# Six gate blocks of each layer computed with the first six mixer units instead of in the merge

## The chip, the cores and the metric

The kernel runs on one core of a Trainium2 chip. The metric is device time in microseconds for one execution of the whole program, the median of three runs. TensorE (PE) multiplies, VectorE (DVE), ScalarE (ACT) and GpSimd (POOL) do the element-wise work, and SyncE (SP) issues every DMA.

## The reference, cut to what matters

Two layers of a hybrid backbone over 640 tokens (512 latent, 128 prompt) of width 1024. In each layer the normed input h is projected once; the columns feed three token mixers (A, B, C) and 24 gate blocks of 128 channels (8 for each branch).

```
z = h @ w_in_l
gates = sigmoid(g + b_gate_l)                       # 3 branches x 1024 channels
y = gates[:, :, 0] * (oa @ w_ba) + gates[:, :, 1] * (ob @ w_bb) + gates[:, :, 2] * (oc @ w_bc)
x = x + mp[2] * (y @ w_o)                           # then an MLP of the squared ReLU
```

A gate block depends on h alone. It is needed only where the branch product of the same 128 channels is multiplied by it.

## The kernel before, in words

Every product is computed to nearly float32: both operands are split into a high and a low float32r part, and three matmuls (high x high, high x low, low x high) make one. A block of 128 output channels over 640 tokens with 8 input blocks is therefore 8 x 3 x 2 = 48 matmuls, one of 256 and one of 384 columns in each pair (`HALVES`, `product`, lines 34 and 818).

**Weights** come in one stream in the order of use (`Stream`, line 535): `_program` gives its order, `load` fetches a piece of up to 768 columns, `make` splits pieces of 384 columns into high (ACT, `act`) and low. In the mixers the low part is made by POOL (`ws.lo = "POOL"`, lines 1290 and 1311), in the merge and the MLP by DVE (line 1341). The split pieces live in a circle of 10 x 384 columns; `ws.hold` keeps pieces that are read again.

**Mixers** (lines 1310 to 1338). Ten units, four of A, two of B, four of C. For each unit the eight weight pieces of 384 columns are held while five tiles of 128 tokens are projected (`Unit.project`, 24 matmuls of 384 columns each) into PSUM banks 0 and 1 (`zb`), and evacuated by ACT, DVE and POOL. Then `step` advances the attention jobs of this unit and of the two before it: scores, softmax, transposes, the product with v. Results go to DRAM (`ospill`).

**Merge** (lines 1341 to 1391). For each of three branches b: four blocks of the mixers' result are fetched from `ospill` into places of `gy` and split by POOL (high) and DVE (low) into `og`; then eight gate blocks (48 matmuls each, a tanh on ACT into a place of `gy`); then eight branch products over `og` (24 matmuls each), which DVE multiplies by 1 + gate and adds up. The places of `gy` lie in the mixers' memory (`U0`, `U1A`, `U1C`), so none of them in U0 can be written before the mixers' last use of U0. PSUM banks 0 to 5 are taken in turn, two for each block. At each gate block and at each branch product one step of `later` is issued (line 736): it loads 512 KB of modulation weights and multiplies and sums them on DVE with two custom instructions (line 294, 32 steps in a layer, two buffers). Before that, `conditioning` (line 647) makes the vector that these steps need, on ACT and DVE.

After the merge come the output projection, a norm and the MLP.

**Order.** The program's operations are not issued as written: `Plan.schedule` (line 167) simulates the engines with fixed durations, and each engine takes the ready operation with the lowest number, its place in the program plus a bias (`FILL` puts projections back, `EVAC` puts evacuations forward). The order that comes out is fixed; on the chip each engine runs it as it stands.

Of the kernel before, what the change touches and what calls it, by code (L numbers as in the profile page):

```python
# [39 lines left out]
SLACK = 0  # L40
FILL = {"A": 0, "B": 450, "C": 200}
LAST = 3
PRE = 2
LAG = 3
ORDER = (0, 1, 4, 2, 3)
LAM_INIT = [0.8 - 0.6 * math.exp(-0.3 * l) for l in range(DEPTH)]


# [361 lines left out]
def _program():  # L410

    r = []

    def cols(n):
        if r and r[-1][0] == "n":
            r[-1][1] += n
        else:
            r.append(["n", n])

    for l in range(DEPTH):  # L420
        r.append(["layer", 0])
        cols(NU * KT * UW + 3 * (KT * D + KT * 512) + D * KT)
        for kind, n, f in _mlp_order():
            if kind == "s":
                r += [["s", j] for j in range(7)]
            elif kind == "2":
                for d in range(KT):
                    r.append(["m", MLP_GROUPS[n] * P])
                    if d < 7:
                        r.append(["s", d])  # L430
            else:
                cols(n * D if kind == "1" else MLP_GROUPS[n] * D)
    return r
# [3 lines left out]
@with_exitstack  # L437
def hybrid_step(ctx: ExitStack, tc: tile.TileContext, a: dict):
    nc = tc.nc
    pool = ctx.enter_context(tc.tile_pool(name="sb", bufs=1))  # L440
    ppool = ctx.enter_context(tc.tile_pool(name="ps", bufs=1, space=PSUM))
    dpool = ctx.enter_context(tc.tile_pool(name="dr", bufs=1, space=DRAM))
    mf = pool.tile([P, F_WORDS], F32, name="mf")
    mr = pool.tile([P, R_WORDS], F32R, name="mr")
    scratch_nc = _bacc.Bacc("TRN2", target_bir_lowering=False, num_devices=1)
    scratch = ctx.enter_context(tile.TileContext(scratch_nc))
    psm = ppool.tile([P, 8, 512], F32, name="psm")
    xspill = dpool.tile([KT, P, T], F32, name="xspill")
    ospill = dpool.tile([12, P, T], F32, name="ospill")
    pl = Plan(nc)  # L450

    def view(place, words):
        with scratch.tile_pool(name="names", bufs=1) as names:
            return pl.view(pool, names, place, words)

    hybrid_plan(pl, a, mf, mr, view, psm, xspill, ospill)
    with tc.manual_schedule():
        pl.issue()
    return pl


def hybrid_plan(pl, a, mf, mr, view, psm, xspill, ospill):
    mm, tp, act, tt, ts, stt = pl.mm, pl.tp, pl.act, pl.tt, pl.ts, pl.stt
    perf, perr = Bump(mf, 0, F_WORDS), Bump(mr, 0, R_WORDS)

# [387 lines left out]
    class Phase1:  # L853
        def __init__(self):
            b, r = fmem(), rmem()
            self.hl = r.ring(768, 2)
            self.pt = r.slots(512, 10)
            self.pp = b.slots(T, 10)
            self.bias = b.tile(2048)
            self.ck, self.cv = b.tile(256), b.tile(128)  # L860
            self.zc = b.tile(UW)
            self.tmp = b.ring(320, 5)
            u0, u1a, u1b, u1c = [f32r(view(*x)) for x in (("U0", UNIT0), ("U1A", UNIT1A), ("U1B", UNIT1B), ("U1C", UNIT1C))]
            self.q = [u0[:, :2560], u1a[:, :2560]]
            self.kk = [u0[:, 2560:3840], u1c[:, :1280]]
            self.v = [u0[:, 3840:5376], u1b[:, :1536], u0[:, 5376:6912]]
            self.kp = [u1b[:, 1536:1792], u1b[:, 1792:2048]]
# [440 lines left out]
    for l in range(DEPTH):  # L1308
# [5 lines left out]
        def step(i):  # L1314

            for j in (i - 2, i, i - 1):
                if 0 <= j < len(jobs):
                    next(jobs[j], None)

        n = 0  # L1320
        for u in range(NU):
            un = Unit(l, u, ph)
            un.cached()
            if l == 0 and u == 0:
                for t in ORDER:
                    un.evacuate(first_z[t], t)
            else:
                ws.hold = ws.cur
                W = [ws.get(UW, 1) for _ in range(KT)]
                ws.hold = None  # L1330
                for t in ORDER:
                    un.project(W, t)
            for job in un.jobs():
                jobs.append(job)
                step(n)
                n += 1
# [15 lines left out]
        for b in range(3):  # L1352
            og = []
            for i in range(4):
                bo, of = gy.get()
                pl.dma(of, ospill[4 * b + i], keys_in=[("o", 4 * b + i, 0), ("o", 4 * b + i, NLAT)])
                oh, ol = oss.get(), oss.get()
                pl.pts(oh, of, 1.0, 0.0, ALU.mult, ALU.add)
                tt(ol, of, f32(oh), ALU.subtract)
                gy.put(bo)  # L1360
                og.append((oh, ol))
            gs = []
            for d in range(KT):
                outs = product(pb, hpairs)
                g = gy.get()
                for z, (c0, c1) in zip(outs, HALVES):
                    act(g[1][:, c0:c1], z[:, :c1 - c0], AF.Tanh, scale=0.5, bias=bgate[:, l, b * 8 + d:b * 8 + d + 1])
                gs.append(g)
                run(later, 1)
            if b == 2:  # L1370
                for k in range(KT):
                    if l == 0:
                        pl.dma(xs[k], a["x"][k])
                    else:
                        pl.dma(xs[k], xspill[k], keys_in=[("x", k)])
            for d in range(KT):
                outs = product(pb, og)
                bg, g = gs[d]
                run(later, 1)
                for z, (c0, c1) in zip(outs, HALVES):  # L1380
                    stt(g[:, c0:c1], g[:, c0:c1], 1.0, z[:, :c1 - c0], ALU.add, ALU.mult)
                    if b:
                        tt(ys[d][1][:, c0:c1], ys[d][1][:, c0:c1], g[:, c0:c1], ALU.add)
                if b == 0:
                    ys[d] = gs[d]
                else:
                    gy.put(bg)
                if b == 2:
                    act(hh[d], ys[d][1], AF.Copy)
                    tt(hl[d], ys[d][1], f32(hh[d]), ALU.subtract)  # L1390
# [176 lines left out]
def _kmajor(w, c0, c1):  # L1567

    k = w.shape[0] // P
    return w[:, c0:c1].reshape(k, P, c1 - c0).transpose(1, 0, 2).reshape(P, -1)  # L1570
# [13 lines left out]
def _stream(i):  # L1584
    parts, pairs = [], []
    for l in range(DEPTH):
        w_in = i["w_in"][l]
        for u in range(NU):
            parts.append(_kmajor(w_in[:, _unit_cols(u)], 0, UW))
        for b, n in enumerate(("w_branch_a", "w_branch_b", "w_branch_c")):  # L1590
            for d in range(KT):
                c = 3840 + b * D + d * P
                parts.append(_kmajor(w_in, c, c + P))
            for d in range(KT):
                parts.append(_kmajor(i[n][l], d * P, (d + 1) * P))
        for k0, k1 in ((0, KT - LAST), (KT - LAST, KT)):
            for d in range(KT):
                parts.append(_kmajor(i["w_out"][l][k0 * P:k1 * P], d * P, (d + 1) * P))
        f0s = np.cumsum((0,) + MLP_GROUPS)
        w1 = i["w_ff1"][l]  # L1600

        def pair(f0):
            b = [_kmajor(w1, f * P, (f + 1) * P).reshape(P, 4, 2, P) for f in (f0, f0 + 1)]
            pairs.append([b[f][:, :, k].reshape(P, SW) for f, k in ((0, 0), (0, 1), (1, 0), (1, 1))])

        for kind, n, f0 in _mlp_order():
            if kind == "1":
                for f in range(n):
                    parts.append(_kmajor(w1, f * P, (f + 1) * P))
            elif kind == "s":  # L1610
                pair(n)
            else:
                for d in range(KT):
                    parts.append(_kmajor(i["w_ff2"][l][f0s[n] * P:f0s[n + 1] * P], d * P, (d + 1) * P))
                if kind == "2":
                    pair(f0)
    flat = np.concatenate(parts, axis=1)
    out, at, np_ = [], 0, 0
    for kind, n in _program():
        if kind == "n":  # L1620
            for c in range(0, n, CW):
                out.append(flat[:, at + c:at + min(c + CW, n)].ravel())
            at += n
        elif kind == "m":
            out.append(flat[:, at:at + n].ravel())
            at += n
        elif kind == "s" and n == 0:
            out += [x.ravel() for x in pairs[np_]]
            np_ += 1
    assert at == flat.shape[1] and np_ == len(pairs)  # L1630
    return np.concatenate(out).astype(np.float32)
# [100 lines left out]
```

## Time and profile before

| | us |
|---|---|
| median of three runs | 2399.0 (2398.05 to 2400.93) |
| the profiled execution | 2395.86 |
| its span, first to last instruction | 2394.1 |

The span is cut at the places where the work changes. In layer 0 the mixers run to about 485 us and the merge follows to about 720; in layer 1 the mixers run from about 1200 to 1650. A line of the windows view gives, for a stretch, its length, then each engine's busy time with its number of instructions, the granted clock of TensorE as a share of full speed, the DMA share and the GB/s.

### The profile page before, as it was taken

The page shows a single profiled execution, that of the slowest core. Times are in us where ns is not written, and L with a number is a line of the kernel's source. Part 1 is how long each engine was busy: PE and PEld are TensorE (multiplying, and loading weights), DVE is VectorE, ACT ScalarE, POOL GpSimd, SP SyncE. Part 2 cuts the span into 40 slices and gives each one's busy share as a digit, 9 for nine tenths or more (in the row PEclk, how much of TensorE's full clock was granted, in tenths as well). Part 3 has the DMA queues.
Part 4 walks back from the last instruction along what each step waited for, and adds up shares of the span by engine and source line. Part 5 has one row for each costly group of instructions (what it writes and reads, how often), then busy time and mean ns, then how long its engine had stood idle before and what let it go on. Part 6 is the DMA issues. An engine that isn't in the chain of part 4 may idle for free. (4 is left out here: it accounts for less than half of the span.)

```text
span 2394.1 us, 41963 instructions
## 1 busy us (share of the span) xinstructions
PE 2331.1 (97%) x15476; PEld 2271.7 (95%) x15476; DVE 1817.3 (76%) x3993; ACT 1212.5 (51%) x2810; POOL 433.7 (18%) x513
## 2 busy tenths in 40 slices
PE   8999999999999999999999999999999999999997
PEld 7898999999999999999989998999999999999997
DVE  7778878789746999877678787777983687777776
ACT  4565678632233644444476667765222363544442
POOL 3436534200000000000045454331000000000000
PEclk9999999999999999999999999999999999999998
DMA  7212112476422244322241112226662222222222
GB/s 251 89 43 66 48 47 86 147 234 211 139 73 71 79 134 142 102 83 71 82 133 57 45 51 69 68 91 223 206 201 80 78 64 69 80 81 84 84 71 67
DMA packets 104753, 245.39 MB, mean 102 GB/s; under 512 B 12770, under 2 KB 24546, under 8 KB 103524
## 3 DMA queue, kind: packets, MB, share of 16 engines
q1 hardware_dynamic: 104548, 242.71, 32.5%
q8 instruction: 122, 2.00, 0.3%
q14 instruction: 83, 0.68, 0.1%
HBM read 225.62 MB, written 17.04 MB: 101 GB/s over the span
## 5 line engine op out<-in xcount | busy, mean ns | idle before, releaser
L245 PE MATMUL psm<-mr 128*128 128x384 f32 (+2 forms) x10784 | 1807.4, 319 | 17.7 <-ACT mr L262 6.5
L245 PEld LDWEIGHTS psm<-mr 128*128 128x128 f32 x10784 | 1658.8, 189 | 26.1 <-ACT mr L262 7.8
L262 ACT ACTIVATE mr<-mf 128x384 fp32r<-128x384 f32 (+4 forms) x956 | 470.9, 514 | 675.4 <-PE psm L245 583.5
L267 DVE TENSOR_TENSOR mr<-mf,mr 128x384 fp32r<-128x384 f32 (+5 forms) x802 | 445.4, 567 | 172.5 <-ACT mr L262 167.5
L311 POOL TENSOR_TENSOR mf<-mf 128x5 f32<-128x5 f32 (+3 forms) x85 | 85.1, 1001 | 1234.2 <-DVE mf L267 1229.8
L280 DVE SCALAR_TENSOR_TENSOR mf<-psm,mf 128x256 f32<-128x256 f32 (+3 forms) x588 | 211.3, 403 | 112.6 <-PE psm L245 103.0
L262 ACT ACTIVATE mf<-mf 128x320 f32<-128x320 f32 (+6 forms) x401 | 192.0, 499 | 104.1 <-DVE mf L267 59.7
L294 DVE CUSTOM_DVE_ANT_0 psm<-mf,U1B 128x1024 f32<-128x1024 f32 x160 | 197.6, 1235 | 14.3 <-DMA mf<-wmod 13.4
L305 POOL TENSOR_SCALAR mf<-mf 128x640 f32<-128x640 f32 (+3 forms) x236 | 144.8, 617 | 349.9 <-DVE mf L267 290.2
L262 ACT ACTIVATE mf<-psm,mf 128x640 f32<-128x640 f32 (+3 forms) x256 | 162.4, 643 | 63.9 <-DVE mf L267 47.6
L311 POOL TENSOR_TENSOR mr<-mf,mr 128x384 fp32r<-128x384 f32 x162 | 180.7, 1135 | 63.7 <-ACT mr L262 63.0
L267 DVE TENSOR_REDUCE mf<-psm 128x1 f32<-128x640 f32 (+2 forms) x212 | 148.2, 703 | 38.4 <-PE psm L245 32.9
L245 PE MATMUL psm<-U,mr 128*128 128x320 f32 (+1 forms) x1110 | 174.5, 305 | 0.6 <-ACT mr L262 0.5
L245 PEld LDWEIGHTS psm<-U,mr 128*128 128x128 f32 x1110 | 163.5, 189 | 1.2 <-ACT mr L262 0.6
L267 DVE TENSOR_TENSOR mr<-psm,mr 128x512 fp32r<-128x512 f32 (+2 forms) x252 | 140.9, 578 | 25.0 <-ACT mr L262 22.3
L245 PE MATMUL psm<-U1A,mr 128*128 128x256 f32 (+2 forms) x814 | 152.9, 309 | 0.0
L262 ACT ACTIVATE mr<-psm 128x512 fp32r<-128x512 f32 (+2 forms) x252 | 123.5, 513 | 53.4 <-PE psm L248 45.6
L267 DVE TENSOR_TENSOR mf<-mf 128x512 f32<-128x512 f32 (+8 forms) x269 | 139.4, 528 | 13.6 <-POOL mf L305 5.9
L245 PEld LDWEIGHTS psm<-U1A,mr 128*128 128x128 f32 x814 | 132.2, 188 | 0.0
L248 PE MATMUL psm<-mf 128*128 128x128 f32 x752 | 120.9, 277 | 4.6 <-DVE mr L267 2.6
L267 DVE TENSOR_TENSOR mf<-psm,mf 128x128 f32<-128x128 f32 (+4 forms) x240 | 91.5, 397 | 37.9 <-ACT mf L262 23.0
L262 ACT ACTIVATE mf<-psm 128x320 f32<-128x320 f32 (+8 forms) x188 | 76.1, 410 | 78.5 <-PE psm L245 74.3
(93 smaller groups left out, 1700.1 us busy)
## 6 DMA issues: line engine op xcount, KB each, us to landing
mf<-w SPq DMA_DIRECT2D x232, 384.0 KB, 3.1
mf<-wmod SPq DMA_DIRECT2D x84, 512.0 KB, 3.9
mf<-w SPq DMA_DIRECT2D x156, 256.0 KB, 2.7
U1C<-w SPq DMA_DIRECT2D x48, 256.0 KB, 2.7
mf<-bias SPq DMA_DIRECT2D x8, 1024.0 KB, 5.3
U<-wmod SPq DMA_DIRECT2D x12, 512.0 KB, 6.6
mf<-x SPq DMA_DIRECT2D x16, 320.0 KB, 4.5
ospill<-mf SPq DMA_DIRECT2D x16, 256.0 KB, 2.9
```

The lines of the kernel that those rows point to most:

```text
L245: self.add("PE", d, lambda R: self.nc.tensor.matmul(R(out), R(lhsT), R(rhs), start=start, stop=stop), [out], [lhsT, rhs])
L248: self.add("PE", 55 if in_.dtype == F32R else 108, lambda R: self.nc.tensor.transpose(R(out), R(in_), ident), [out], [in_, ident])
L262: self.add("ACT", d, lambda R: self.nc.scalar.activation(R(out), R(in_), func, **kw), outs, ins)
L267: self.add("DVE", d, lambda R: getattr(self.nc.vector, name)(R(out), *map(R, ins), *args, **kw), [out] + list(extra), list(ins) + [x for x ...
L280: self.add("DVE", d, lambda R: self.nc.vector.scalar_tensor_tensor(R(out), R(a), s, R(b), op0, op1), [out], [a, b] + ([s] if hasattr(s, "a ...
L294: self.add("DVE", d, lambda R: self.nc.vector.tensor_tensor_reduce(out=R(out), in0=R(a), in1=R(b), scale=1.0, scalar=0.0, op0=ALU.mult, op ...
L305: self.add("POOL", d, lambda R: self.nc.gpsimd.tensor_scalar(R(out), R(a), s1, s2, op0, op1), [out], [a] + [s for s in (s1, s2) if hasattr ...
L311: self.add("POOL", d, lambda R: self.nc.gpsimd.tensor_tensor(R(out), R(a), R(b), op), [out], [a, b])
```

## The change

Gate blocks 0 to 5 of each layer (six of the eight of branch A) are computed in the mixers, block i right after the projection of unit i, with the projection's two PSUM banks, one half of the tokens after the other. The tanh goes to a small ring in the memory that the C units' bias uses later, and from there by DMA to a DRAM buffer `gspill`. In the merge these six blocks are fetched from `gspill` into their places of `gy`; the step of `later` that belongs to each stays. The weight stream is put in the new order.

```diff
@@ _program
-        cols(NU * KT * UW + 3 * (KT * D + KT * 512) + D * KT)
+        for u in range(NU):
+            r.append(["n", KT * UW])
+            if u in EARLY:
+                r.append(["n", D])
+        r.append(["n", 3 * (KT * D + KT * 512) + D * KT - len(EARLY) * D])
@@ class Phase1
             self.pp = b.slots(T, 10)
+
+            self.gate = Ring(mf, b.at, PW, 5)
             self.bias = b.tile(2048)
@@ mixers
+        def early_gate(l, i, p):
+
+            blks = []
+            for hf, (c0, c1) in enumerate(HALVES):
+                ws.hold = ws.cur if not hf else ws.hold
+                pl.bias = GATE
+                z, = product(zb, hpairs, (hf,), blks, 1)
+                pl.bias = 0
+                g = p.gate.get()[:, :c1 - c0]
+                act(g, z[:, :c1 - c0], AF.Tanh, scale=0.5, bias=bgate[:, l, i:i + 1])
+                pl.dma(gspill[i, :, c0:c1], g, keys_out=[("g", i, c0)])
+            ws.hold = None
...
                 for t in ORDER:
                     un.project(W, t)
+            if u in EARLY:
+                early_gate(l, EARLY.index(u), ph)
             for job in un.jobs():
@@ merge
             for d in range(KT):
+                g = gy.get()
+                if b * 8 + d < len(EARLY):
+                    i = b * 8 + d
+                    pl.dma(g[1], gspill[i], keys_in=[("g", i, 0), ("g", i, 256)])
+                    gs.append(g)
+                    run(later, 1)
+                    continue
                 outs = product(pb, hpairs)
-                g = gy.get()
```

`EARLY` is (0, 1, 2, 3, 4, 5) and `GATE` is 0. `_stream` lays the weights out in the same order.

## Rows read from the trace of the kernel before

**Rows 1.** The page: engine totals, and TensorE's granted clock in 40 slices of the span (tenths).

```profile
PE 2331.1 (97%) x15476; PEld 2271.7 (95%) x15476; DVE 1817.3 (76%) x3993; ACT 1212.5 (51%) x2810; POOL 433.7 (18%) x513
...
PEclk9999999999999999999999999999999999999998
```

**Rows 2.** Windows of layer 0: the mixers while the first units run, their middle, their last 23 us; then the merge: six gate blocks of branch A, its eight products, the eight gate blocks of branch B, its eight products.

```profile
55.00:350.00 295.00, 278.62 (x1781) 263.50 (x1780) 229.75 (x559) 186.35 (x489) 141.23 (x165) 0.97 0.19 60
350.00:462.00 112.00, 110.66 (x722) 103.16 (x721) 85.08 (x227) 82.30 (x221) 39.21 (x55) 1.00 0.31 101
462.00:485.00 23.00, 22.88 (x166) 22.36 (x165) 17.56 (x45) 13.88 (x34) 4.81 (x8) 1.00 0.68 232
485.00:527.00 42.00, 42.00 (x289) 42.00 (x288) 35.41 (x59) 17.37 (x34) 3.87 (x4) 1.00 0.68 216
527.00:555.00 28.00, 28.00 (x193) 28.00 (x192) 27.15 (x53) 5.78 (x11) 3.79 (x4) 1.00 0.65 201
555.00:611.00 56.00, 56.00 (x384) 56.00 (x383) 49.95 (x90) 18.04 (x37) 1.59 (x1) 1.00 0.70 224
611.00:639.00 28.00, 28.00 (x193) 28.00 (x192) 24.42 (x51) 5.78 (x11) 2.98 (x4) 1.00 0.42 134
```

**Rows 3.** Windows of layer 1: the mixers while the first units run, their last 23 us, and the products of branch B.

```profile
1215.00:1500.00 285.00, 270.31 (x1742) 253.15 (x1742) 224.97 (x550) 189.75 (x498) 144.78 (x169) 0.99 0.21 67
...
1627.00:1650.00 23.00, 22.89 (x164) 22.40 (x164) 17.23 (x43) 14.16 (x35) 5.62 (x8) 1.00 0.70 234
...
1776.00:1804.00 28.00, 28.00 (x193) 28.00 (x192) 25.61 (x53) 5.78 (x11) 2.96 (x4) 1.00 0.49 156
```

**Rows 4.** Waits of TensorE from 55 to 462 us, the three longest in total: us, times, longest.

```profile
PE psm L245 <- ACT mr L262: 4.5, 4, 2.2
PE psm L248 <- DVE mr L267: 4.2, 7, 1.8
PE psm L245 <- POOL mr L311: 2.8, 2, 2.4
```

**Rows 5.** Groups of TensorE's instructions by shape, 462 to 484.9 us: the products of gate blocks that run in the mixers' last 23 us.

```profile
L245 PE MATMUL psm<-mr 128*128 128x384 f32 x42 | 11.0, 347 | 0.0
L245 PE MATMUL psm<-mr 128*128 128x256 f32 x54 | 10.5, 289 | 0.0
```

**Rows 6.** TensorE's timeline at the end of the mixers: the first run of gate matmuls that nothing interrupts, in layer 0 and in layer 1 (start, length, count).

```profile
484.96 15.24 PE L245 MATMUL psm<-mr 128*128 128x256 f32 x103
...
1649.83 22.34 PE L245 MATMUL psm<-mr 128*128 128x384 f32 x151
```

**Rows 7.** Timelines of SP, POOL and DVE: the four blocks of branch A's input are fetched (SP), split into high (POOL) and low (DVE), layer 0 and then layer 1; before the DVE rows, the work on U1B that `conditioning` puts there.

```profile
485.15 1.75 SPq L317 DMA_DIRECT2D U<-ospill  x4
...
490.82 2.57 POOL L305 TENSOR_SCALAR mr<-U 128x640 fp32r<-128x640 f32 x3 [15.50 <-DMA U<-ospill]
494.21 1.44 POOL L305 TENSOR_SCALAR mr<-U 128x640 fp32r<-128x640 f32 x1 [0.82 <-DMA U<-ospill]
...
488.65 1.23 DVE L280 SCALAR_TENSOR_TENSOR U1B<-psm,U1B 128x1024 f32<-128x1024 f32 x1 [1.68 <-ACT psm L262]
...
493.86 1.21 DVE L294 CUSTOM_DVE_ANT_0 psm<-mf,U1B 128x1024 f32<-128x1024 f32 x1
...
494.99 3.53 DVE L267 TENSOR_TENSOR mr<-U,mr 128x640 fp32r<-128x640 f32 x4
...
1654.79 4.09 POOL L305 TENSOR_SCALAR mr<-U 128x640 fp32r<-128x640 f32 x4 [14.35 <-DMA U<-ospill]
...
1657.39 0.90 DVE L267 TENSOR_TENSOR mr<-U,mr 128x640 fp32r<-128x640 f32 x1
...
1661.96 0.81 DVE L267 TENSOR_TENSOR mr<-U,mr 128x640 fp32r<-128x640 f32 x1
```

**Rows 8.** The same four fetches of layer 0: time from issue to landing.

```profile
DMA to landing us min/median/max: 5.5/6.3/7.7
```

**Rows 9.** Groups of DVE's instructions by shape. First the custom instructions of the modulation steps (two to a step) with their accumulator reads from 527 to 555 us; then the custom ones from 555 to 611 with the low parts split there; then the same two from 611 to 639.

```profile
L294 DVE CUSTOM_DVE_ANT_0 psm<-mf,U1B 128x1024 f32<-128x1024 f32 x16 | 20.3, 1269 | 0.3 <-DMA mf<-wmod 0.3
...
L294 DVE DVE_READ_ACCUMULATOR2_ANT mf<- 128x1 f32 x15 | 2.1, 139 | 0.0
...
L294 DVE CUSTOM_DVE_ANT_0 psm<-mf,U1B 128x1024 f32<-128x1024 f32 x29 | 35.8, 1233 | 2.1 <-DMA mf<-wmod 1.9
...
L267 DVE TENSOR_TENSOR mr<-U1A,mr 128x640 fp32r<-128x640 f32 x3 | 2.3, 827 | 0.0
...
L294 DVE CUSTOM_DVE_ANT_0 psm<-mf,U1B 128x1024 f32<-128x1024 f32 x5 | 6.1, 1225 | 0.0
...
L267 DVE TENSOR_TENSOR mr<-U1C,mr 128x640 fp32r<-128x640 f32 x2 | 2.6, 1338 | 0.0
```

**Rows 10.** Windows around a place in the mixers where TensorE stands still for some microseconds: that place, and a stretch soon after it.

```profile
223.00:234.00 11.00, 7.93 (x39) 7.14 (x40) 9.30 (x25) 4.77 (x13) 10.17 (x12) 0.82 0.35 111
...
241.00:248.00 7.00, 7.00 (x53) 6.97 (x52) 4.45 (x13) 4.44 (x15) 0.67 (x2) 1.00 0.03 9
```

**Rows 11.** Groups by shape: the low and high parts of weight pieces as POOL and ACT make them from 55 to 350 us; and, from 485 to 527 us, the tanh of gate blocks.

```profile
L311 POOL TENSOR_TENSOR mr<-mf,mr 128x384 fp32r<-128x384 f32 x57 | 65.4, 1165 | 22.3 <-ACT mr L262 22.0
...
L262 ACT ACTIVATE mr<-mf 128x384 fp32r<-128x384 f32 x56 | 27.4, 517 | 2.2 <-PE psm L245 2.1
...
L262 ACT ACTIVATE U<-psm,mf 128x384 f32<-128x384 f32 x7 | 4.0, 575 | 0.0
L262 ACT ACTIVATE U<-psm,mf 128x256 f32<-128x256 f32 x7 | 3.3, 468 | 4.4 <-PE psm L245 4.4
```

More of the change, by code (lines that the diff above doesn't have):

```diff
@@ L42 @@
 LAST = 3
+GATE = 0
 PRE = 2
@@ L45 @@
 ORDER = (0, 1, 4, 2, 3)
+EARLY = (0, 1, 2, 3, 4, 5)
 LAM_INIT = [0.8 - 0.6 * math.exp(-0.3 * l) for l in range(DEPTH)]
@@ L449, in hybrid_step @@
     ospill = dpool.tile([12, P, T], F32, name="ospill")
+    gspill = dpool.tile([len(EARLY), P, T], F32, name="gspill")
     pl = Plan(nc)
@@ L454, in view @@
             return pl.view(pool, names, place, words)
-    hybrid_plan(pl, a, mf, mr, view, psm, xspill, ospill)
+    hybrid_plan(pl, a, mf, mr, view, psm, xspill, ospill, gspill)
     with tc.manual_schedule():
@@ L459, in hybrid_step, with hybrid_plan @@
     return pl
-def hybrid_plan(pl, a, mf, mr, view, psm, xspill, ospill):
+def hybrid_plan(pl, a, mf, mr, view, psm, xspill, ospill, gspill):
     mm, tp, act, tt, ts, stt = pl.mm, pl.tp, pl.act, pl.tt, pl.ts, pl.stt
@@ L1587, in _stream @@
         w_in = i["w_in"][l]
+        gate = lambda g: _kmajor(w_in, 3840 + g * P, 3840 + (g + 1) * P)
         for u in range(NU):
             parts.append(_kmajor(w_in[:, _unit_cols(u)], 0, UW))
+            if u in EARLY:
+                parts.append(gate(EARLY.index(u)))
         for b, n in enumerate(("w_branch_a", "w_branch_b", "w_branch_c")):
-            for d in range(KT):
-                c = 3840 + b * D + d * P
-                parts.append(_kmajor(w_in, c, c + P))
+            for g in range(max(b * KT, len(EARLY)), (b + 1) * KT):
+                parts.append(gate(g))
             for d in range(KT):
```

## The prediction

> **What bounds the kernel now.** I read the page first: TensorE is busy for 97% of the span at nearly full clock [rows 1], so the time is its work plus its gaps, and a change that moves work without removing any can only win in gaps. Then the windows by stage, to see where the gaps are. In the merge there are none: 42, 28, 56 and 28 us are busy to the last hundredth [rows 2]. In the mixers, while the first units run, TensorE stands 295.00 - 278.62 = 16.4 us in layer 0 [rows 2] and 285.00 - 270.31 = 14.7 us in layer 1 [rows 3]; in the next 112 us only 1.3 [rows 2]. Last I read what stands beside TensorE at the seam of mixers and merge, because there the removed blocks are today's cover [rows 5 to 8].
>
> **The sum of the moved work is zero.** From 485 to 527 us TensorE does nothing but gate blocks: 289 matmuls in 42.00 us [rows 2], 0.145 us each, so a block of 48 is 7.0 us and six are 42 us in a layer. They leave the merge, where TensorE is full, and so the merge gets 42 us shorter if nothing new is late. The same matmuls enter the mixers, which get 42 us longer less what falls into gaps. Four terms remain, for one layer.
>
> **1. Gaps filled in the mixers: 6 us gained.** The ceiling is the idle time of the first units, 16.4 and 14.7 us [rows 2, 3]. Not all of it can be had. Of layer 0's waits 4.5 us end with a high part from ACT and 2.8 with a low part from POOL [rows 4]: there TensorE waits for weight pieces, and a gate block draws on the same stream. What a gate block can fill are the waits of transposes for their split inputs (4.2 us, [rows 4]) and the small ones. The block also stands ahead of the unit's attention steps in the program, and so runs as a lump right after the projection and not as filler spread over the unit. The other end is a loss: the lump holds up the steps for 7 us. DVE has 65 us of 295 free there [rows 2] and can catch up, so I put that at no more than 3 us. I take 6, nearer to the fillable waits than to the whole idle time; the bounds are 3 lost to 16 gained. Beside it, and hidden, are 16 more pieces to split for six blocks (1024 columns each, 384 to a piece): POOL 16 x 1.165 = 18.6 us and ACT 16 x 0.517 = 8.3 us [rows 11], and twelve tanh of 0.47 to 0.58 us [rows 11], on engines busy for 141 and 186 of 295 us [rows 2]. The split circle holds 3840 columns; a unit with its gate block asks for 4096, so the next unit's pieces start only as the projection's last tile lets go of old ones. The 7 us of the gate block are the cover for that. Twelve small writes to DRAM queue on SP behind nothing that is late.
>
> **2. The cover at the seam: 10.5 us lost.** The mixers' last 23 us are filled with 42 + 54 = 96 gate matmuls [rows 5], exactly two blocks. After the change blocks 6 and 7 are the two that are left, and they fill it as before. But then TensorE has nothing. Today it goes on with six gate blocks at 484.96 us [rows 6]; afterwards the next in turn is branch A's first product, which needs all four pieces of `og`. The next branch's gate blocks can't step in, since PSUM banks and weights are taken in turn. The four fetches go out at 485.15, when U0 comes free, and take 5.5 to 7.7 us [rows 7, 8]; POOL starts at 490.82, DVE at 494.99 after the conditioning work, and ends at 498.52 [rows 7]. Four more matmuls and a handshake put the product's end near 499.3, where without a wait it would end at 484.96 + 24 x 0.145 = 488.4: 10.9 us. In layer 1 the last split ends at 1662.77 [rows 7], which gives 1663.6 against 1649.83 + 3.5 = 1653.3 [rows 6]: 10.3 us. I take 10.5. If DVE took the pieces as soon as they landed it would be some 6.5 (first landing 5.5, then 4 x 0.88 of DVE and a POOL split), with a slower landing 13. Today this chain costs nothing, since 42 us of gate blocks lie over it. The six fetches from `gspill` queue behind these on SP; at the latter's 7.7 us they land by about 500, before DVE first needs one.
>
> **3. The clock: 2 us lost.** Where TensorE was busy for 7.93 of 11 us the mean granted clock was 0.82, and it was 1.00 again a few us later [rows 10]. A stand of 10 us should bring the lower level (1.2 GHz) too, and some of it will reach past the stand. At 0.82 of 11 us about 4 us are at half speed, which is worth 2; bounds 0 and 6.
>
> **4. DVE in branch B's products: 5 us lost.** The modulation steps do not keep pace with TensorE, they run at their own: 16 custom instructions in 28 us, 29 in 56 [rows 9], so a step (two of them) every 3.7 us, from 493.86 on [rows 7], in the merge's first two branches. In branch A's products that already lies beside TensorE without a gap (DVE 27.15 of 28, [rows 2]), so they stay whole. But branch B's products will come earlier: 485 + 10.5 + 28 + 56 = 580 instead of 611. By then 86 / 3.7 = 23 steps are done and not 30, and some 8 of the 32 fall beside these products, where today there are 2.5 [rows 9]. A step is 2 x (1.23 + 0.14) = 2.7 us [rows 9], so DVE is asked for 24.42 + 5.5 x 2.7 = 39 us in 28 [rows 2]. Three products can wait in PSUM, and the gate blocks after them ask little of DVE, which takes up most of the 11. I take 5, between 0 and 14 (no PSUM room, a ninth step). The low parts that DVE no longer splits (16 pieces) were in the first branch and free nothing here.
>
> **Sum.** -6 + 10.5 + 2 + 5 = +11.5 us a layer, 23 in two. The profiled execution took 2395.9 (span 2394.1 and 1.8 around it), so 2419 there; the median of the runs is 3.1 above it, so 2422.
>
> **A rule that speaks against the change.** Two low parts of 640 columns took DVE 1338 ns each in the stretch where POOL works beside them, three took 827 where POOL had one instruction [rows 9, 2]. The Trainium skill, in "SBUF — State Buffer" (SBUF: two separate sides), says that VectorE with two SBUF inputs and GpSimd reading SBUF exclude each other, one waiting for the other's whole instruction. By that rule, the trace agrees, the 16 splits that move to POOL would hold up DVE in the mixers.
>
> **The rivals.**
> - *DVE held up by POOL in the mixers.* 16 splits a layer, half a microsecond each by the two durations above [rows 9], all on the chain to TensorE: 8 us a layer, 2438. Against it: DVE has slack there [rows 2]. Chance 0.08.
> - *The steps crowd branch A's products.* Six steps are issued with no gate block under them; if they all run ahead of the products' evacuations, 6 x 2.7 = 16 us, less half in PSUM: 8 us a layer, 2438. Against it: two buffers hold the steps to one in 3.7 us [rows 9]. Chance 0.12.
> - *The gates don't fill.* They run as lumps and the idle time stays: term 1 is 0, 2434. Chance 0.13.
> - *The gates fill nearly all (faster).* Idle time in the first units goes whole, 16.4 and 14.7 us, at the waits of transposes and evacuations, while the seam costs 6.5 to 10.5 and the rest nothing: about -4.5 to -9 a layer, 2381 to 2390. It decides once the fill passes the seam's cost, about 10 us a layer. For it: the idle time is there [rows 2, 3]. Against it: half of it waits for the weight stream [rows 4]. Chance 0.12.
> - *Even.* Fill of 10 against the seam alone: about 2399. Chance 0.10.
>
> **How the numbers follow.** The forecast has 0.45. A measurement of this kernel can tell about 0.2%, 4.8 us, from no change. Faster is the fourth rival, 0.12; within it the fifth, 0.10; the rest, 0.78, is slower. The bounds of the terms alone give -9.5 to +36 a layer; the range for 8 in 10 goes from 2398 (most of the even case in, the faster one out) to 2446 (both 2438 rivals in, their sum out).
>
> **What would show it.** Right: the mixers longer by about 36 us a layer; a wait of TensorE of about 10 us after the last matmul of the mixers that ends with branch A's low parts on DVE; the clock under 1.00 there; DVE near 28 of 28 in branch B's products with TensorE waiting for it. Wrong: no such wait at the seam, or mixers longer by less than 30 us; either makes the change even or a gain.

## The result, and the profile after

The median after is 2435.1 us (2432.3 to 2437.4) against 2399.0 before: a ratio of 1.0147, 95% interval 1.0135 to 1.0159, so 36 us slower. Both are medians of four runs. The forecast was 2422 in a range of 2398 to 2446.

The profiled span is 2431.9 us, 37.8 longer. TensorE's totals on the page of the changed kernel, to be held against [rows 1]: the same 15476 matmuls, 12.7 us more busy, 25 us more idle.

```profile
span 2431.9 us, 41955 instructions
...
PE 2343.8 (96%) x15476; PEld 2275.2 (94%) x15476; DVE 1807.5 (74%) x3961; ACT 1212.6 (50%) x2814; POOL 464.1 (19%) x549
```

Where the layers end shows in the view of one tensor: the first layer writes its result for the second to DRAM from 1205.8 us before and from 1224.1 after, so 18.3 us are lost in layer 0 and 19.5 in layer 1.

```profile
L317 SPq DMA_DIRECT2D xspill<-mf x8: 319/320/442, 1205.8 to 1218.1; - x8
```

```profile
L320 SPq DMA_DIRECT2D xspill<-mf x8: 319/320/353, 1224.1 to 1236.5; - x8
```

The fetch of branch A's input marks the seam of mixers and merge. Before, it goes out at 485.15 [rows 7] and, in layer 1, at 1650.02; after, at 528.14 and 1712.41. SP's timeline, layer 1 before, then both layers after:

```profile
1650.02 1.75 SPq L317 DMA_DIRECT2D U<-ospill  x4
```

```profile
528.14 1.75 SPq L320 DMA_DIRECT2D U<-ospill  x4
...
1712.41 1.75 SPq L320 DMA_DIRECT2D U<-ospill  x4
```

The mixers of layer 0 are 43.0 us longer, those of layer 1 62.4 - 18.3 = 44.1. The moved matmuls are worth 42. So the mixers lose 1 to 2 us a layer, and the rest of each layer's loss, about 17 us, lies in the merge.

Windows of the changed kernel (columns as in [rows 2]): the mixers of layer 0; the seam; branch A's products; B's eight gate blocks; B's products; the mixers of layer 1.

```profile
55.00:528.00 473.00, 454.07 (x2942) 427.74 (x2940) 340.01 (x828) 296.62 (x774) 201.40 (x246) 0.99 0.27 83
528.00:540.00 12.00, 5.67 (x21) 5.16 (x21) 9.20 (x11) 4.22 (x6) 3.92 (x4) 0.64 1.00 364
540.00:564.00 24.00, 24.00 (x160) 24.00 (x160) 21.36 (x42) 4.73 (x9) 0.22 (x1) 0.96 0.56 180
564.00:620.00 56.00, 56.00 (x384) 56.00 (x384) 51.09 (x92) 16.75 (x35) 4.51 (x4) 1.00 0.68 217
620.00:658.00 38.00, 33.53 (x227) 32.52 (x226) 36.25 (x70) 6.09 (x12) 4.53 (x4) 1.00 0.66 206
...
1233.00:1712.00 479.00, 460.11 (x2980) 430.49 (x2979) 336.49 (x836) 307.81 (x803) 203.01 (x251) 1.00 0.27 85
```

Read the first against [rows 2]: before, TensorE stood 16.4 + 1.3 + 0.1 = 17.8 us between 55 and 485; after, 473.00 - 454.07 = 18.9 between 55 and 528. The same for layer 1, where the kernel before has

```profile
1215.00:1650.00 435.00, 418.01 (x2703) 390.43 (x2703) 335.48 (x836) 292.71 (x773) 191.50 (x234) 1.00 0.26 83
```

that is 17.0, and 18.9 after. Six more blocks of work ran in each layer's mixers, and the sum of the idle time did not fall. Its parts did change. TensorE's waits in the mixers of layer 0 after (the first, second and sixth in total), against [rows 4]:

```profile
PE psm L251 <- DVE mr L270: 5.0, 10, 1.2
PE psm L248 <- DVE mf L283: 3.4, 3, 1.5
...
PE psm L248 <- ACT mr L265: 1.3, 1, 1.3
```

The waits of matmuls for low parts from POOL (2.8 us in layer 0, 1.4 in layer 1) are gone, and those for high parts from ACT fell from 4.5 to 1.3 in layer 0. The waits for VectorE rose in their place, from 9.1 to 13.4 us in layer 0.

The seam: in 12 us TensorE did 21 matmuls, which at 0.145 us are 3; then 160 in 24 us, 0.7 us short of full: 9.7 us lost. Branch B's products: 227 in 38 us, 33.0 us at full rate: 5.0 lost. What TensorE waited for, 528 to 700 us:

```profile
PE psm L248 <- POOL mr L308: 5.5, 1, 5.5
PE psm L248 <- DVE U L283: 3.3, 3, 1.7
PE psm L248 <- DVE U1A L283: 1.1, 1, 1.1
PE psm L248 <- DVE mr L270: 0.8, 1, 0.8
```

The first and last are branch A's split pieces at the seam, the other two the products with the gates in branch B (line 283 is `stt`). The waits alone make 10.7 of the 14.7 us. Most of the rest lies in matmuls at the lower clock: 26 of them took 7.26 us, and at 0.145 us each they would take 3.8. TensorE's timeline at the seam, VectorE's last two low parts of branch A, and the clock in windows cut to the seam:

```profile
526.43 1.68 PE L248 MATMUL psm<-mr,U 128*128 128x512 f32 x10 [0.50 <-DVE mr L270]
533.65 1.97 PE L248 MATMUL psm<-mr 128*128 128x256 f32 x6 [5.53 <-POOL mr L308]
536.41 8.80 PE L248 MATMUL psm<-mr 128*128 128x256 f32 x42 [0.80 <-DVE mr L270]
```

```profile
538.68 1.55 DVE L270 TENSOR_TENSOR mr<-U,mr 128x640 fp32r<-128x640 f32 x2
```

```profile
531.50:541.70 10.20, 7.26 (x26) 6.86 (x27) 9.49 (x12) 1.55 (x2) 3.92 (x4) 0.50 0.87 321
541.70:546.00 4.30, 4.30 (x31) 4.30 (x31) 2.69 (x5) 1.05 (x2) 0.00 (x0) 1.00 0.39 122
```

A wait of 5.5 us, and for 10.2 us around it the lower of the two clock levels, 1.2 GHz, past the wait until about the end of branch A's first product.

The windows place 14.7 of the 17 us that the merge of layer 0 lost. The 42 us after them lose another 0.7; the rest is not placed.

### The profile page after: what moved, and what is told of

Read it like the earlier page. It is cut to its first block, busy times and chain, and to the rows that moved or that the text cites. A ratio compares the mean times of both kernels' runs of the same rounds, so it can differ in the third digit from the quotient of the medians.

```text
span 2431.9 us, 41955 instructions
## 1 busy us (share of the span) xinstructions
PE 2343.8 (96%) x15476; PEld 2275.2 (94%) x15476; DVE 1807.5 (74%) x3961; ACT 1212.6 (50%) x2814; POOL 464.1 (19%) x549
## 4 chain that ended last, share of the span: by engine, by line
PE 83%; DVE 9%; ACT 3%; issue 2%; POOL 1%; DMA 1%; SPq 0%; POOLq 0%; ACTq 0%; DVEq 0%
PE psm L248 78%; PE psm L251 5%; DVE mr L270 3%; DVE mf L270 2%; ACT mr L265 1%; DVE mf L283 1%; DVE psm L297 1%; ACT mf L265 1%; POOL mf L314 1%; DVE U L270 1%; DMA mf<-wmod 1%; ACT U L265 1%; DVE U1C L297 0%; DVE U1B L270 0%; DMA mf<-x 0%
## 5 line engine op out<-in xcount | busy, mean ns | idle before, releaser
L248 PE MATMUL psm<-mr 128*128 128x384 f32 (+2 forms) x10784 | 1825.9, 320 | 38.3 <-POOL mr L308 10.0
L248 PEld LDWEIGHTS psm<-mr 128*128 128x128 f32 x10784 | 1665.8, 190 | 51.7 <-DVE mr L270 11.3
L265 ACT ACTIVATE mr<-mf 128x384 fp32r<-128x384 f32 (+5 forms) x960 | 466.9, 512 | 650.5 <-PE psm L248 518.1
L270 DVE TENSOR_TENSOR mr<-mf,mr 128x384 fp32r<-128x384 f32 (+5 forms) x770 | 432.3, 577 | 152.9 <-ACT mr L265 147.4
L314 POOL TENSOR_TENSOR mr<-mf,mr 128x384 fp32r<-128x384 f32 (+1 forms) x198 | 207.9, 1069 | 524.7 <-ACT mr L265 516.7
L314 POOL TENSOR_TENSOR mf<-mf 128x256 f32<-128x256 f32 (+3 forms) x85 | 87.0, 1024 | 823.6 <-DVE mf L270 816.2
L265 ACT ACTIVATE mf<-psm,mf 128x640 f32<-128x640 f32 (+3 forms) x280 | 175.3, 633 | 74.9 <-DVE mf L270 54.8
L270 DVE TENSOR_TENSOR mf<-mf 128x512 f32<-128x512 f32 (+8 forms) x269 | 135.7, 514 | 13.4 <-ACT mf L265 6.1
L251 PEld LDWEIGHTS psm<-mr 128*128 128x128 f32 x600 | 73.2, 141 | 43.5 <-DVE mr L270 23.0
```

Source lines behind the costliest of these rows:

```text
L248: self.add("PE", d, lambda R: self.nc.tensor.matmul(R(out), R(lhsT), R(rhs), start=start, stop=stop), [out], [lhsT, rhs])
L251: self.add("PE", 55 if in_.dtype == F32R else 108, lambda R: self.nc.tensor.transpose(R(out), R(in_), ident), [out], [in_, ident])
L265: self.add("ACT", d, lambda R: self.nc.scalar.activation(R(out), R(in_), func, **kw), outs, ins)
L270: self.add("DVE", d, lambda R: getattr(self.nc.vector, name)(R(out), *map(R, ins), *args, **kw), [out] + list(extra), list(ins) + [x for x ...
L314: self.add("POOL", d, lambda R: self.nc.gpsimd.tensor_tensor(R(out), R(a), R(b), op), [out], [a, b])
```

## The experiments

Two questions were open: what holds the merge up, and why the mixers' idle time took none of the work. The 12 runs are given in that order. "Before" is measured again beside each set (2398.0 to 2400.2 us).

**Early blocks taken from another branch.** `e1_branch_c` makes the first six blocks of branch C early, and no block of A or B; `e2_branch_b` the first six of B (`FIRST = 8`).

```diff
+FIRST = 16
-                act(g, z[:, :c1 - c0], AF.Tanh, scale=0.5, bias=bgate[:, l, i:i + 1])
+                act(g, z[:, :c1 - c0], AF.Tanh, scale=0.5, bias=bgate[:, l, FIRST + i:FIRST + i + 1])
...
-                if b * 8 + d < len(EARLY):
-                    i = b * 8 + d
+                if FIRST <= b * 8 + d < FIRST + len(EARLY):
+                    i = b * 8 + d - FIRST
```

(The weight stream follows in `_stream`.) Expected of e1:

> The six early blocks are the first six of branch C (16 to 21) and not of branch A; everything else is as changed. Theory S: the mixers grow by about 43 us a layer whichever blocks are made there, the merge shrinks by 42, and all of the rest of the loss (about 17 us a layer) is the uncovered seam and VectorE in branch B's products; with branch A's and B's blocks back in place both vanish, so 2402 us (2398 to 2407). Rival R: the merge has no room for the moved work wherever it is taken out (fetches, modulation steps crowd it), so about 2435. Rival F: the gaps of the mixers are filled and only hidden by the seam, so under 2394.

Measured: 2399.5 us, ratio 1.0008 (0.9999 to 1.0017). The time is in theory S's range: with the merge's first two branches left whole, all but 1.6 of the 36 us are back. The mixers filled nothing here either (rows below).

> The six early blocks are the first six of branch B (8 to 13). Theory S: all eight blocks of branch A lie over the seam again, so its 11 to 12 us a layer go, but branch B's products come as early as in the changed kernel and VectorE holds them up by 5 to 6 us a layer: 2402 + 11 = 2413 us (2408 to 2418), with waits of TensorE for VectorE's products with the gates in that stage and none at the seam. If VectorE's share is no cause of its own: 2402. If the seam is not the cause: about 2435.

Measured: 2432.6 us, ratio 1.0146 (1.0132 to 1.0159), as slow as the change, and the sum of S is wrong. There is no wait at the seam; nearly the whole loss sits in B's products (211 matmuls in 46 us are 15 us short of full). Windows of e2: B's products, and all from the seam to the end of B's products; then TensorE's waits from 525 to 700 us.

```profile
614.00:660.00 46.00, 33.64 (x211) 31.82 (x210) 44.23 (x85) 6.88 (x15) 4.41 (x4) 0.93 0.70 218
...
531.00:660.00 129.00, 116.64 (x777) 114.82 (x776) 118.95 (x216) 31.78 (x64) 13.17 (x12) 0.97 0.69 218
...
PE psm L249 <- DVE U L284: 7.4, 6, 1.8
PE psm L249 <- DVE U1A L284: 4.9, 1, 4.9
```

VectorE is busy for 44.23 of 46 us there.

**The seam's wait taken away.** `e3_seam` changes the order of `gy`'s places, so that branch A's input goes to memory that comes free earlier.

```diff
-        gy = Pieces(tiles((view("U0", UNIT0), 11), (view("U1A", UNIT1A), 4), (view("U1C", UNIT1C), 2)))
+        gy = Pieces(tiles((view("U1A", UNIT1A), 4), (view("U0", UNIT0), 11), (view("U1C", UNIT1C), 2)))
```

> The changed kernel with the places of gy in another order (U1A's four first), so that branch A's four blocks of mixer results are fetched to memory that comes free some 13 us before U0. Theory S with the fetch as the seam's price: the fetch leaves the chain, splitting and conditioning stay, the wait shrinks by 4 to 9 us a layer, 2417 to 2427 us. Rival: conditioning on ACT and DVE, or the buffers of the split parts, set the end and the fetch is hidden behind them: 2432 to 2438 with the wait as it is.

Measured: 2429.5 us, ratio 1.0133 (1.0120 to 1.0147). The wait at the seam is gone altogether, more than expected, and yet only some 5 of 36 us came back (36.2 above before, now 31.6). Most of the seam's 10 us a layer appears in B's products instead, where TensorE now waits 5.0 + 4.8 us for VectorE in layer 0 against 3.3 + 1.1:

```profile
PE psm L248 <- DVE U1A L283: 5.0, 3, 2.9
PE psm L248 <- DVE U L283: 4.8, 1, 4.8
```

So the two places of the loss are not two causes to be added. In the changed kernel the first two branches take 130 us from the seam on, in e2 129:

```profile
528.00:658.00 130.00, 119.20 (x785) 117.67 (x785) 117.91 (x213) 31.80 (x62) 13.18 (x12) 0.96 0.68 220
```

TensorE's own work there is 112 us (two stages of products of 28 us and eight gate blocks of 7). VectorE is asked for 118, most of it modulation steps that start only behind the seam and come one in 3.7 to 3.8 us. That led to theory D: these steps bound the first two branches, wherever the wait shows.

**The steps spread out.** `e7_spread` issues a step in two of three places over all three branches, in the changed kernel; `e8_seam_spread` does the same in e3.

```diff
+        slots = iter(range(6 * KT))
+
+        def some():
+            if next(slots) % 3 < 2:
+                run(later, 1)
...
-                run(later, 1)
+                some()
```

> The changed kernel with the 32 modulation steps of a layer spread over all three branches of the merge (two in every three places) and not over the first two. Theory D (e2 and e3 showed that covering the seam alone gives the loss back in branch B's products: VectorE's work in the first two branches, most of it modulation steps, is what bounds them now): the waits in branch B's products go, 5 to 6 us a layer, the seam stays: 2422 to 2427 us. If those waits are not the steps' doing: 2433 to 2437.

> e3_seam (the early-free memory first, so no wait at the seam) together with the spread steps of e7_spread. Theory D: both causes are gone, nothing is given back, and only the mixers' growth without fill is left: 2400 to 2406 us, as e1_branch_c. Rival (a third cause in the merge, such as the fetches of the stored gates): over 2412.

Measured: 2422.3 us for e7 (ratio 1.0092, 1.0079 to 1.0106) and 2401.5 for e8 (1.0008, 0.9999 to 1.0017). Both as D says. TensorE's waits of e7 from 525 to 700 us show the seam as before and none for the products with the gates:

```profile
PE psm L248 <- POOL mr L308: 5.5, 1, 5.5
PE psm L248 <- DVE mr L270: 1.7, 2, 1.2
```

With the steps spread, removing the seam's wait is worth 21 us; without, some 5. In e8 the same stretch is 112 us and without a gap:

```profile
533.00:645.00 112.00, 112.00 (x766) 112.00 (x765) 102.47 (x189) 31.03 (x61) 8.92 (x8) 1.00 0.66 213
```

No third cause that these runs can resolve (they tell about 5 us) is left in the merge, the fetches of the stored gates included.

**Why nothing is filled.** All that follows makes C's blocks early, as e1 does, to have the merge out of the way. First the gate matmuls are put back in the planner's order (`GATE = 600`):

> As e1_branch_c, with the matmuls of the early blocks put 600 places back in the planner's order, so that they stand behind the attention steps and serve as filler. Theory L (they fill nothing because they run as a lump right after the projection): 6 to 12 us below e1_branch_c. Theory H (the idle time lies at hand-overs that are later on the chip than the fixed order allows for, and more filler changes nothing): within 4 us of e1_branch_c.

Measured: 2398.2 us, ratio 1.0001 (0.9992 to 1.0009), within 4 us of e1. The edit moved little: in layer 0 the first matmuls of 256 columns of a block start within 3 us of where they do in e1, but for one unit (255.6 us and not 250.3). What speaks against theory L more is the trace of the changed kernel, in which the blocks are no lumps to begin with. From 202.2 to 213.2 us the 24 matmuls of 256 columns of one block lie between 39 matmuls of the attention steps and 17 transposes:

```profile
L248 PE MATMUL psm<-U1B,mr 128*128 128x256 f32 x39 | 5.8, 287 | 0.0
L248 PE MATMUL psm<-mr 128*128 128x256 f32 x24 | 3.9, 292 | 0.0
...
L251 PE MATMUL psm<-mr 128*128 128x128 f32 x12 | 1.9, 236 | 0.0
```

Then the planner is told that what TensorE gets from another engine comes later (`SLACK = 150`), with the early blocks (e5) and in the kernel before (e6):

> As e1_branch_c, with the planner told that anything TensorE gets from another engine comes 150 ns later than it assumes, so that the fixed order puts more work of its own between. Theory H (idle time sits at hand-overs that come later on the chip than in the order): the gate blocks now have gaps to go to, TensorE's idle time in the mixers falls from about 18 to under 12 us a layer, and the kernel is 6 to 20 us below e1_branch_c, about 2385 to 2393. Rival (idle time is set by another engine's throughput, VectorE's above all, and no order helps): within 4 us of e1_branch_c or slower.

> The kernel before, with the same 150 ns in the planner and no early gate blocks: the control for e5_slack. If the 150 ns alone are what helps, it gains as much against before as e5_slack against e1_branch_c. If the gate blocks are the filler that the order lacks, it gains less than e5_slack, or loses, since there is nothing to put into the gaps but what was there: within 5 us of before.

Measured: e5 2387.4 us, ratio 0.9947 (0.9935 to 0.9960), 12 us below e1 (14 when each is held against the "before" of its own set) and faster than before; e6 2408.5, ratio 1.0036 (1.0024 to 1.0048), slower by 8, more than the 5 that were expected at most. The same 150 ns cost 8 us without the early blocks and bring 12 to 14 with them. Windows of the mixers, layer 0 and layer 1, of e1, e5 and e6:

```profile
55.00:528.70 473.70, 455.20 (x2951) 430.14 (x2950) 341.30 (x828) 296.62 (x773) 203.43 (x246) 0.99 0.26 84
1216.00:1694.70 478.70, 460.74 (x2995) 431.40 (x2994) 336.80 (x837) 307.83 (x803) 203.35 (x251) 1.00 0.27 85
```

```profile
55.00:521.80 466.80, 452.05 (x2961) 429.56 (x2960) 336.63 (x827) 297.05 (x773) 199.50 (x246) 0.99 0.27 85
1209.40:1683.00 473.60, 460.90 (x3004) 433.52 (x3003) 338.87 (x838) 307.40 (x802) 204.36 (x251) 1.00 0.27 86
```

```profile
55.00:496.60 441.60, 419.54 (x2684) 397.76 (x2683) 334.87 (x828) 282.93 (x744) 183.57 (x228) 0.97 0.24 78
1223.80:1664.90 441.10, 420.40 (x2714) 395.97 (x2713) 339.05 (x837) 293.08 (x773) 191.32 (x235) 0.98 0.25 82
```

TensorE's idle time in the two layers is 18.5 and 18.0 us in e1, 14.8 and 12.7 in e5, 22.1 and 20.7 in e6, where the kernel before has 17.8 and 17.0. It fell, but not under 12 us as expected of e5. The mixers of e5 are 6.9 and 5.1 us shorter than e1's, which is nearly the whole gain of its profiled execution. So in the mixers the early blocks are a filler, but only when the fixed order leaves room at the hand-overs; there the allowance without filler makes new gaps.

That inputs come later than the order assumes shows in one place at least. The planner counts (66 + 128) / 0.96 = 202 ns for a low part of 128 columns on VectorE (`vec`); in the mixers of the changed kernel they take 274 to 1137 ns (rows at the end of this section). How late the hand-overs themselves are was not measured.

More of it:

> e5_slack with 300 ns in the planner. Theory H with hand-overs later than 150 ns as well: 2378 to 2385. If 150 ns cover what the chip is late by, or the supply of filler is used up: 2385 to 2395.

> e5_slack with 450 ns in the planner. If hand-overs are later than 300 ns on the chip too and the supply of filler holds: another 4 to 10 us below e11_slack300, 2366 to 2372. If the supply is used up, or the order now keeps TensorE's inputs waiting for longer than they are late: 2374 to 2385.

Measured: e11 2376.3 us, ratio 0.9908 (0.9893 to 0.9923), below its expected range; e12 2372.0, ratio 0.9893 (0.9877 to 0.9910), 4.3 below e11, at the near end of its first case. Against the "before" of their own sets, 150, 300 and 450 ns give 13, 24 and 26 us: each step brings less. Whether the supply of filler is used up or the lateness covered, no run shows. Mixers of e12:

```profile
55.00:519.00 464.00, 451.03 (x2984) 433.67 (x2983) 337.86 (x827) 295.64 (x775) 201.98 (x245) 0.99 0.27 86
1202.60:1670.80 468.20, 457.85 (x3017) 435.85 (x3017) 335.56 (x837) 306.76 (x803) 203.01 (x251) 1.00 0.27 88
```

They are 464 and 468 us long where e1's are 474 and 479, with 13.0 and 10.4 us idle. That is 20 of the 28 us between the profiled executions of e1 and e12; the other 8 lie outside the mixers, where no block was added, so there the allowance pays without filler. 300 and 450 ns without early blocks were not run. e12 beats both kernels, by 1.1% and 2.6%.

> e5_slack with the early blocks' matmuls put 600 places back as in e4. If the blocks run as lumps even with the 150 ns in the order, putting them back frees more gaps: 2378 to 2384. If the 150 ns alone place them well: within 3 us of e5_slack (2387).

Measured: 2391.5 us, ratio 0.9967 (0.9954 to 0.9979), 4 us above e5 and outside both cases; the two intervals just overlap. Putting the blocks back brings nothing here either.

**GpSimd's extra splits.** `e9_dve_low` splits the low parts of the early blocks' weights on VectorE, in e1 (`gates` holds the numbers of their pieces).

```diff
-                if self.lo == "POOL":
+                if self.lo == "POOL" and i not in self.gates:
```

> As e1_branch_c, with the low parts of the early blocks' weight pieces split by VectorE as in the merge and not by GpSimd: 16 instructions of 0.55 us a layer on VectorE for 16 of 1.1 us on GpSimd. If GpSimd's extra work in the mixers holds VectorE up on the way to TensorE (the rival of the prediction), 8 us a layer come back: about 2384. If neither is on the chain: 2396 to 2402.

Measured: 2396.5 us, ratio 0.9989 (0.9981 to 0.9998) against e1's 1.0008 (0.9999 to 1.0017): about 2 us a layer on average, not 8. In its profiled execution the gain is all in layer 0.

There is such an effect on VectorE. Its low parts of 128 columns with both inputs in SBUF, 34 in the mixers of layer 0, in the kernel before, after, and in e9:

```profile
L267 DVE TENSOR_TENSOR mr<-mf,mr 128x128 fp32r<-128x128 f32 x34 | 14.4, 423 | 2.1 <-ACT mr L262 2.0
```

```profile
L270 DVE TENSOR_TENSOR mr<-mf,mr 128x128 fp32r<-128x128 f32 x34 | 16.8, 495 | 1.6 <-ACT mr L265 1.2
```

```profile
L271 DVE TENSOR_TENSOR mr<-mf,mr 128x128 fp32r<-128x128 f32 x34 | 13.3, 390 | 1.0 <-ACT mr L266 0.7
```

But the amount of GpSimd's work does not decide: in layer 1 the same three means are 363, 448 and 452 ns. What decides is whether a GpSimd instruction runs at that moment. After, in layer 0, the 16 of the 34 that no GpSimd instruction overlaps took 278 to 292 ns; the other 18 took 683 on average and up to 1137. VectorE and GpSimd in the changed kernel, at one such place:

```profile
284.42 0.28 DVE L270 TENSOR_TENSOR mf<-psm,mf 128x128 f32<-128x128 f32 x1
284.62 0.68 DVE L270 TENSOR_TENSOR mr<-mf,mr 128x128 fp32r<-128x128 f32 x1
...
284.11 1.06 POOL L308 TENSOR_SCALAR mf<-mf 128x640 f32<-128x640 f32 x1 [1.19 <-DVE mf L270]
```

The low part ends at 285.30, just behind the GpSimd instruction (285.17). The instruction ahead of it has one input in PSUM and keeps its 0.28 us beside the same GpSimd instruction. So do the 86 low parts of 512 columns that read PSUM: 686 ns on average beside a GpSimd instruction, 685 without. The rule in the Trainium skill, "SBUF — State Buffer" (SBUF: two separate sides), that a VectorE instruction with two SBUF inputs and a GpSimd instruction that reads SBUF exclude each other, agrees with these rows. The price in the kernel is a quarter of what the rival had.

## Why the prediction was right or wrong

The direction and the two places of the loss in the merge were right, and the time lay in the range. The sum was 13 us short of the 36, and the first term alone accounts for it.

**Gaps filled, "6 us gained": failed.** The mixers lost 1 to 2 us a layer, so the term was off by 7 to 8, 15 us in two layers. I priced the idle time as a supply that more work can draw on, and discounted it for weight waits and for the lump. Both discounts were misplaced. The blocks ran as no lump (202.2 to 213.2 us above), and the waits for weight pieces, which I took to be out of reach, are the ones that shrank, while the waits for VectorE, which I took to be fillable, grew. The order of each engine is fixed from assumed durations, so where an input comes later than assumed TensorE stands before it, whatever other work is behind; new hand-overs took the place of the old ones, and the idle time stayed. e5, e11 and e12 show it from the other side: with the lateness allowed for, the mixers with the same blocks are 5 to 10 us a layer shorter (e5 and e12 against e1). That the lateness is the cause is argued from what the allowance did and from the 202 ns above; it was not measured at the hand-overs. In layer 0 the blocks also came as 18 more pieces to split, 12 of 384 and 6 of 256 columns, and not 16; with their low parts on VectorE (e9) some 2 us a layer come back, about what the mixers lost.

**The seam, 10.5 us, and the clock, 2 us: 9.7 together in layer 0.** The chain was the forecast one: fetch, high parts, conditioning, low parts. But the wait was not one of 10 us that ends with a low part. It was 5.5 us up to the first high part from POOL and 0.8 up to a low part; the rest of the loss is 26 matmuls at 1.2 GHz. VectorE's last low part of branch A ended at 540.23, so at the higher clock the first product could not have ended before that, and at the lower one it ended at about 541.2 (541.7 less two matmuls of 0.27 us). From these rows I estimate the clock's own price at under 1 us; no run separates it.

**VectorE in branch B's products, 5 us: 5.0 in layer 0 as far as 658 us.** Ten steps fell there (20 custom instructions), where eight were forecast. Place and size were right.

**The sum of these was near, 17.5 against about 17 lost and 14.7 placed, but for a reason that I had not seen.** I added them as separate prices; that the sum came out is in part luck. e2 and e3 show that they share one floor: from the seam to the end of B's products all three kernels need 125 to 130 us, in which VectorE is busy for 115 to 119; TensorE's work is only 112, and what the seam doesn't take B's products do. Had the seam been covered, I would have forecast 25 us back (12.5 a layer), and it would have been some 5.

**The rivals.** The gates that don't fill (2434) came nearest to the time, with the wrong reason: not the lump. The steps crowding branch A's products did not come: from 540 us on that stage lost 0.7 us. GpSimd in VectorE's way is real and small. The faster rival needed the idle time to be had as it stood, which it was not.

## What to carry to other kernels

Idle time between hand-overs in a fixed order is not free room. In these mixers work put there filled it only once the order allowed for late hand-overs, and an allowance of 150 ns paid there only with work to put in, so the two are tried together. Before work is taken out of a full stage, add up every engine's work in the stage that is left. Here VectorE's 118 us stood against 112 of TensorE's, and covering one wait only moved it. Take the work from the stage where the other engines have the most room (here branch C, some 34 us better than branch A for as many blocks).

## What the runs showed of the hardware that was not expected

One wait of 5.5 us brought the lower clock level for 10.2 us (granted clock 0.50 from 531.5 to 541.7 us), while shorter waits in the mixers left it at 1.00 for most of the time. VectorE's low parts of 128 columns with both inputs in SBUF took 278 to 292 ns (16 of 34, layer 0 of the changed kernel) with no GpSimd instruction beside them and 683 on average with one, while an instruction with one input in PSUM kept its 0.28 us.
